# One decoder block with 32 routed experts: the overflow branch ahead of the first expert pair, a hand-ordered router, the last pair's w1 in alternating pieces, and the first FFN splits on the vector engine

## The chip, the cores and the metric

The program runs on one core of a Trainium2 chip. The metric is the device time of one execution in microseconds (us). The kernel before took 915.79 us as the median of three runs (914.03 to 917.89). The engines are named as in the profile: PE is the tensor engine's matrix multiply and PEld its weight load, DVE the vector engine, ACT the scalar engine, POOL the GpSimd engine, and SP the engine whose queue issues the DMAs.

## What is computed

256 tokens of width 1024 pass through two blocks in float32. The first block has a mixer (retention and a gated delta rule), an output projection, and a mixture of experts; the second has a pooling mixer and a convolutional feed-forward network (FFN) of hidden width 2816. The parts that matter here:

```
mod = silu(c) @ w_ada + b_ada                       # shifts, scales, gates
x = x + gate1 * (mix @ w_out)
h2 = modulate(rmsnorm(x), shift2, scale2)
# router: top 1 of 4 groups, then top 2 of the 8 experts in that group
ys = (silu(xs @ w1[e]) * (xs @ w3[e])) @ w2[e]      # for each token's two experts
x = x + gate2 * segment_sum(ys * gate)
x = rmsnorm(x) ; x = x + pool_mixer(rms_norm(x))
x = x + conv_ffn(rms_norm(x))                       # w_in 1024x5632, 3-tap conv, gate, w_out 2816x1024
```

Each of the 32 experts has w1 and w3 of 1024x512 and w2 of 512x1024, 2 MB each, so that the expert weights are 96 matrices of 2 MB, 201 MB, each read once.

## The kernel before

**Experts.** The 32 experts are worked in 16 pairs (the loop over `p`, L1235). A pair holds 64 slots for each of two experts, 128 rows together. `gather(q)` (L1170) serves two pairs: it builds the one-hot matrix OH from `ranks` on DVE, multiplies the normalised tokens with it (32 matmuls, L1183, with the tokens split in a high and a low part, xh and xl), scales and shifts the result into `xg` on ACT and DVE in turn, and then makes the transposed one-hot matrix `oT` and the slot gates `gs` (L1193 to L1200, called the slot rows below). The pair then multiplies xg with w1 and w3 (L1259), forms `hid` (silu on ACT, product with gs on DVE, L1266), transposes it (L1271) and multiplies with w2 (L1282). The result is split in a high and a low part (L1292 on ACT, L1293 on POOL) and added back to the tokens by `scatter` (L1213, L1217), one pair later.

**Weights.** SP's queue loads each weight matrix into a slot of SBUF (2 MB; eight slots, six from pair 12 on, when `load_tail` rearranges the pools). A slot's DMA waits until the matmuls that read the slot's last weights are done. Pair 0's six matrices and pair 1's w1 are loaded ahead of the experts. The pairs 1, 2 and 3 (FINE) load a matrix in four pieces of 512 KB, which wait for the matmuls of the same quarter; pairs 4 to 14 load each in one DMA of 2 MB; the last pair loads w1 in two DMAs of 2 MB, and w3 and w2 in 512 KB pieces that alternate between its two experts (L1245). The order of PE's and SP's instructions inside the pair loop is that of the code (manual schedule, L1233); elsewhere, and on the other engines, a scheduler sets it.

**The overflow branch.** If an expert has more than 64 tokens, `overflow()` (L1126) works the rest of them with plain loops. Each engine loads the largest count (`bigi`) into a register and branches over the body. With the inputs here the body is skipped. It is called after the w1 and w3 matmuls of pair 1 (L1262). On SP its place is behind the pieces of pair 1's weights.

**Router.** Behind the output projection the logits `lg` give the group (L1066 on), the two experts (L1082 on), their probabilities, and by a prefix sum on PE (L1105 to L1110) each token's rank in its expert. `xl`, the low part of the tokens, is two DVE instructions of 128x1024 (L1116). The scheduler orders them.

**The tail.** After the last pair `stats` (L1326) adds the scattered result, forms v3 (x times the final norm's weight, L1330) and the transposed tokens (L1334); POOL scales the pool weights (L1324); PE multiplies (L1360), ACT and DVE scale the result to `zs` (L1366, L1364), PE sums the windows (L1380), and the result of the normalisation (v3, L1391) is transposed (L1402) and split into gh (ACT) and gl (DVE). The FFN multiplies each weight tile in three parts (L288: high with high, low with high, high with low); ACT makes the high part `wh` of a 128x1024 weight tile (L279), and DVE or POOL the low part `wl` (L282). The first FFN weights, four such tiles, are split in the tail, with wl on POOL (L1374).

Of the kernel before, what the change touches and what calls it, by code (L numbers as in the profile page):

```python
# [177 lines left out]
def build(ctx, tc, io, out, dbg=None):  # L178
# [873 lines left out]
    rinv(ss2[:, :, 0], ss2[:, :, 0], D)  # L1052
    for t in range(2):
        S.activation(xh[:, t, :], x1[:, t, :], AF.Copy, scale=ss2[:, t, 0:1])
    lg = mt([128, 2, 40], "lg")
    for t in range(2):
        V.scalar_tensor_tensor(lg[:, t, :], psl[t][:, 0:40], ss2[:, t, 0:1], rbias, op0=ALU.mult, op1=ALU.add)
# [13 lines left out]
    pg = mt([128, 2], "pg")  # L1071
    V.reciprocal(pg, pz)
# [14 lines left out]
    ez = mt([128, 2], "ez")  # L1087
    for t in range(2):
        S.activation(ee[:, t, :], emx[:, t, :], AF.Exp, bias=enm[:, t:t + 1], accum_out=ez[:, t:t + 1])
    V.reciprocal(ez, ez)  # L1090
    pe = mt([128, 2, 2], "pe")
    V.tensor_tensor(pe, ee[:, :, 0:2], ez[:, :, None].to_broadcast([128, 2, 2]), op=ALU.mult)
# [5 lines left out]
    oh = [mt([128, 2, 32], f"oh{i}") for i in range(2)]  # L1098
    for i in range(2):
        V.tensor_tensor(oh[i], io32[:, None, :].to_broadcast([128, 2, 32]),  # L1100
                        ei[:, :, i:i + 1].to_broadcast([128, 2, 32]), op=ALU.is_equal)
    M = mt([128, 2, 32], "M")
    V.tensor_tensor(M, oh[0], oh[1], op=ALU.add)
    psk = bank()
    PE.matmul(psk[:, 0:32], lhsT=cav("ustrict"), rhs=M[:, 0, :], start=True, stop=True)  # L1105
    PE.matmul(psk[:, 32:64], lhsT=cav("ustrict"), rhs=M[:, 1, :], start=True, stop=False)
    PE.matmul(psk[:, 32:64], lhsT=cav("ones"), rhs=M[:, 0, :], start=False, stop=True)
    psn = bank()
    for t in range(2):
        PE.matmul(psn[:, 0:32], lhsT=cav("ones"), rhs=M[:, t, :], start=t == 0, stop=t == 1)  # L1110
# [3 lines left out]
    V.scalar_tensor_tensor(ranks, psk[:, 0:64].rearrange("p (t e) -> p t e", t=2), 1.0, M, op0=ALU.add, op1=ALU.mult)  # L1114
    for t in range(2):
        V.scalar_tensor_tensor(xl[:, t, :], x1[:, t, :], ss2[:, t, 0:1], xh.bitcast(F32)[:, t, :], op0=ALU.mult, op1=ALU.subtract)  # L1116
    dump("ranks", ranks)
    dump("gates", gates)

# [2 lines left out]
    V.tensor_reduce(big, psn[:, 0:32], axis=AX.X, op=ALU.max)  # L1122
    bigi = mt([128, 1], "bigi", dtype=I32)
    V.tensor_copy(bigi, big)

    def overflow():  # L1126
            nmax = nc.values_load(bigi[0:1, 0:1], min_val=0, max_val=T)
            with tc.If(nmax > SLOTS):
                h2T8 = mt([128, 8, T], "h2T", tag="xg")

                def h2T(k):
                    return h2T8[:, k, :]

                for k in range(8):
                    ps = bank()
                    for t in range(2):
                        for x in (xh, xl):
                            PE.matmul(ps[:, 128 * t:128 * t + 128], lhsT=x.bitcast(F32)[:, t, 128 * k:128 * k + 128], rhs=ident,
                                      start=x is xh, stop=x is xl)
                    affine(h2T(k), ps[:, :T], A2[:, k:k + 1], B2[:, k:k + 1])  # L1140
                gov = mt([128, 2, NE], "gov")
                V.tensor_scalar(gov, ranks, float(SLOTS), None, op0=ALU.is_gt)
                V.tensor_tensor(gov, gov, gates, op=ALU.mult)
                with tc.For_i(0, NE, 1) as e:
                    gcol = mt([128, 2], "gcol")
# [23 lines left out]

    def gather(q):  # L1170

        e0 = 4 * q
        OH = mt([128, 2, 4, SLOTS], "OH", dtype=F32R)
        V.tensor_tensor(OH, cav("iota")[:, None, None, 1:65].to_broadcast([128, 2, 4, SLOTS]),
                        ranks[:, :, e0:e0 + 4, None].to_broadcast([128, 2, 4, SLOTS]), op=ALU.is_equal)
        xg = mt([128, 8, 4 * SLOTS], "xg")
        for d2 in range(4):
            ps = bank("pa").rearrange("p (d s) -> p d s", d=2)
            for d in range(2):
                dd = slice(256 * d2 + 128 * d, 256 * d2 + 128 * d + 128)  # L1180
                for t in range(2):
                    for x in (xh, xl):
                        PE.matmul(ps[:, d, :], lhsT=x[:, t, dd], rhs=OH[:, t].rearrange("p g s -> p (g s)"),  # L1183
                                  start=t == 0 and x is xh, stop=t == 1 and x is xl)
            for d in range(2):
                dd = 2 * d2 + d
                affine(xg[:, dd, :], ps[:, d, :], A2[:, dd:dd + 1], B2[:, dd:dd + 1])
        got = []
        for j in range(2):
            pt = bank("pa")  # L1190
# [1 line left out]
            for t in range(2):  # L1192
                PE.transpose(pt[:, 128 * t:128 * t + 128], oh[t], ident)  # L1193
            for t in range(2):
                PE.matmul(pt[:, T:T + 2], lhsT=oh[t], rhs=gates[:, t, e0 + 2 * j:e0 + 2 * j + 2], start=t == 0, stop=t == 1)
# [35 lines left out]
    last = NE // 2 - 1  # L1231
    order = ExitStack()
    order.enter_context(tc.manual_schedule(engines={ENG.PE, ENG.SP}))  # L1233
    nxt = gather(0)
    for p in range(NE // 2):  # L1235
        if p == 12:
            load_tail()
        for nm in ("w1", "w3", "w2"):
            if p == NE // 2 - 1 and nm != "w1":
                k = 4 if nm == "w2" else 8  # L1240
                for g in range(2):
                    wt[p, nm, g] = slot().rearrange("p a n -> p (a n)").rearrange("p (a n) -> p a n", a=k)
# [128 lines left out]
    for i in range(2):  # L1371
# [107 lines left out]
```

## Time and profile before

The profiled execution took 919.07 us; its span, from the first to the last instruction, is 917.0 us. The table is worked out from the views by stretch.

| stretch (us) | what runs | PE busy | DVE busy | DMA |
|---|---|---|---|---|
| 229 to 253 | end of the output projection, router, first gather | 16.55 of 24 | 14.08 | 36 GB/s |
| 253 to 300 | pairs 0 and 1 | 42.62 of 47 | 8.59 | 324 GB/s |
| 350 to 400 | experts | 50.00 of 50 | 12.57 | 428 GB/s |
| 700 to 730 | pool mixer | 22.89 of 30 | 26.57 | 424 GB/s |
| 760 to 917 | FFN | 153.02 of 157 | 90.21 | 109 GB/s |

A busy PE in the experts is not a PE at its peak: a matmul that is overlapped with the next counts as busy. An answer by line gives, for each group of instructions, the busy time, the mean duration of one, and the idle time of the engine just ahead of it with what ended it.

### The profile page before, as it was taken

What the parts mean: (1) busy time and instruction counts of PE and PEld (TensorE: products, weight loads), DVE (VectorE), ACT (ScalarE), POOL (GpSimd) and SP (SyncE); (2) the same over time, 40 slices, a digit from 0 to 9 for tenths busy, and PEclk for the clock granted to TensorE, in tenths of its full rate; (3) what the DMA queues carried; (4) which work ended last, traced back from release to release, by engine and by line L of the source; (5) the groups of instructions that cost most, each with busy time, mean ns of one, the idle gap of its engine ahead of it and who ended that gap; (6) DMA issues with size and microseconds to landing.
All of it is one profiled execution on the core that took longest, in us unless ns stands there. A gap on an engine that the chain in (4) does not pass through costs nothing. (4 is left out here: it accounts for less than half of the span.)

```text
span 917.0 us, 12931 instructions
## 1 busy us (share of the span) xinstructions
PE 849.2 (93%) x5318; PEld 537.2 (59%) x5318; DVE 402.7 (44%) x739; ACT 274.0 (30%) x505; POOL 195.6 (21%) x141
## 2 busy tenths in 40 slices
PE   3988999989698999999898998999999699999998
PEld 1674778768534435353442533435335599999996
DVE  2577588585512123232122321422206775566554
ACT  2342244454510111011011110211104465555552
POOL 0333331261000111100011010100112424513525
PEclk9997999999799999999999999899999999999999
DMA  9972679768069999999999999999999835454001
GB/s 383 420 323 94 277 283 398 293 258 296 33 225 403 409 419 428 427 428 427 428 425 430 426 430 426 405 404 430 427 410 425 374 111 209 151 226 177 1 1 46
DMA packets 30433, 288.53 MB, mean 315 GB/s; under 512 B 3489, under 2 KB 3873, under 8 KB 15393
## 3 DMA queue, kind: packets, MB, share of 16 engines
q1 hardware_dynamic: 30370, 287.66, 76.8%
q8 instruction: 44, 0.72, 0.3%
q14 instruction: 19, 0.16, 0.0%
HBM read 286.60 MB, written 1.05 MB: 314 GB/s over the span
## 5 line engine op out<-in xcount | busy, mean ns | idle before, releaser
L1259 PE MATMUL ps<-wt,xg 128*64 128x512 f32 x1024 | 237.3, 610 | 14.7 <-DMA wt<-in_w 14.6
L1259 PEld LDWEIGHTS ps<-wt,xg 128*64 128x64 f32 x1024 | 77.7, 140 | 171.3 <-issue 146.1
L279 ACT ACTIVATE wh<-wt 128x512 fp32r<-128x512 f32 (+1 forms) x138 | 114.0, 832 | 98.1 <-PE ps L288 87.7
L1293 POOL TENSOR_TENSOR Yl<-Yf,Yh 128x512 fp32r<-128x512 f32 x30 | 38.3, 1275 | 419.0 <-ACT Yh L1292 419.0
L282 POOL TENSOR_TENSOR wl<-wt,wh 128x512 fp32r<-128x512 f32 (+1 forms) x56 | 106.4, 1912 | 98.7 <-ACT wh L279 96.3
L1282 PE MATMUL ps<-wt,hidT 128*64 128x512 f32 x512 | 113.6, 595 | 0.9 <-ACT hidT L208 0.7
L1266 DVE SCALAR_TENSOR_TENSOR hid<-ps,gs,hid 128x512 f32<-128x512 f32 x16 | 12.0, 751 | 230.6 <-PE ps L1259 202.8
L288 PE MATMUL ps<-gh,wh 128*128 128x256 f32 x352 | 98.8, 281 | 1.4 <-ACT gh L1407 1.4
L288 PE MATMUL ps<-gh,wl 128*128 128x256 f32 x352 | 98.9, 281 | 0.0
L288 PE MATMUL ps<-gl,wh 128*128 128x256 f32 x352 | 98.9, 281 | 0.0
L282 DVE TENSOR_TENSOR wl<-wt,wh 128x512 fp32r<-128x512 f32 (+1 forms) x82 | 79.2, 976 | 44.1 <-ACT wh L279 44.0
L1282 PEld LDWEIGHTS ps<-wt,hidT 128*64 128x64 f32 x512 | 37.3, 137 | 66.4 <-issue 59.4
L288 PEld LDWEIGHTS ps<-gh,wl 128*128 128x128 f32 x352 | 67.6, 192 | 0.0
L288 PEld LDWEIGHTS ps<-gh,wh 128*128 128x128 f32 x352 | 66.0, 188 | 1.8 <-ACT gh L1407 1.6
L288 PEld LDWEIGHTS ps<-gl,wh 128*128 128x128 f32 x352 | 66.1, 188 | 0.2
L1287 DVE TENSOR_TENSOR Yf<-ps,g2b 128x512 f32<-128x512 f32 x31 | 21.4, 692 | 82.2 <-PE ps L1282 82.2
L1292 ACT ACTIVATE Yh<-Yf 128x512 fp32r<-128x512 f32 x30 | 18.9, 630 | 112.6 <-DVE Yf L1287 112.6
L1434 DVE SCALAR_TENSOR_TENSOR yf<-ps,sm,yf 128x254 f32<-128x254 f32 x88 | 41.7, 480 | 12.3 <-ACT yf L1431 10.8
L215 ACT ACTIVATE xg<-ps,modT,A 128x256 f32<-128x256 f32 x32 | 18.1, 565 | 93.1 <-PE ps L1183 93.1
L1265 ACT ACTIVATE hid<-ps 128x512 f32<-128x512 f32 x16 | 9.6, 597 | 112.8 <-PE ps L1259 98.1
L1217 DVE TENSOR_TENSOR x<-x,ps 128x512 f32<-128x512 f32 x64 | 41.2, 681 | 1.3 <-PE ps L1210 0.8
L1438 POOL TENSOR_TENSOR yf<-yf 128x256 f32<-128x256 f32 x22 | 19.6, 893 | 85.2 <-ACT yf L1437 85.2
(380 smaller groups left out, 1307.0 us busy)
## 6 DMA issues: line engine op xcount, KB each, us to landing
wt<-in_w SPq DMA_DIRECT2D x76, 2048.0 KB, 27.3
wt<-in_w SPq DMA_DIRECT2D x80, 512.0 KB, 10.2
wt<-in_w_ada SPq DMA_DIRECT2D x12, 2048.0 KB, 10.6
wt<-in_ffn_w_in SPq DMA_DIRECT2D x11, 2048.0 KB, 8.3
wt<-in_w_in SPq DMA_DIRECT2D x7, 2048.0 KB, 14.0
wt<-in_ffn_w_out SPq DMA_DIRECT2D x5, 2048.0 KB, 9.2
wt<-in_w_out SPq DMA_DIRECT2D x2, 2048.0 KB, 7.9
wt<-in_w_in SPq DMA_DIRECT2D x2, 1024.0 KB, 18.9
```

Of the source, the lines that this page charges most:

```text
L215: S.activation(dst, src, AF.Identity, scale=a, bias=b)
L279: S.activation(hi, src, AF.Copy)
L282: (eng or V).tensor_tensor(lo, src, hi.bitcast(F32), op=ALU.subtract)
L288: PE.matmul(ps, lhsT=a, rhs=b, start=first and n == 0, stop=last and n == 2)
L1217: V.tensor_tensor(a, a, ps[t, c], op=ALU.add)
L1259: PE.matmul(ps[64 * g:64 * g + 64, :], lhsT=xg[:, k, 64 * g:64 * g + 64], rhs=wt[p, nm, g][:, k, :], start=k == 0, stop=k == 7)
L1282: PE.matmul(py[c][64 * g:64 * g + 64, :], lhsT=hidT[:, f, 64 * g:64 * g + 64], rhs=wt[p, "w2", g][:, f, 512 * c:512 * c + 512], start=f == ...
L1287: V.tensor_tensor(yf, py[c], g2b[:, 512 * c:512 * c + 512], op=ALU.mult)
L1292: S.activation(yh, yf, AF.Copy)
L1293: G.tensor_tensor(yl, yf, yh.bitcast(F32), op=ALU.subtract)
L1434: V.scalar_tensor_tensor(y[:, sh:], ps[:, :T - sh], cw[:, 3 * m + tap:3 * m + tap + 1], y[:, sh:], op0=ALU.mult, op1=ALU.add)
L1438: G.tensor_tensor(ys[0], ys[0], ys[1], op=ALU.mult)
```

## The change

Five edits, all in the expert stage and the tail.

1. `overflow()` is called ahead of pair 0, behind the first gather and behind the eight 512 KB pieces of pair 1's w3. Its buffers carry other names; its body is the same.
2. DVE's instructions from the logits to `bigi` follow the order of the code. The order in the code is changed: experts, M and the prefix sums first, then the probabilities, `ranks`, the first OH, then xl, the gates and `bigi`.
3. `gather` is cut in three: `hits` (OH), `gather` (xg) and `slot_rows`. A gather multiplies with all of xh before xl: the first one over all eight column blocks, the later ones two blocks at a time. The slot rows of pairs 0 and 1 are made behind pair 0's w1 and w3 matmuls; those of later gathers stay behind the gather.
4. The last pair's w1 is loaded like its w3, in eight pieces of 512 KB that alternate between the two experts.
5. The four first FFN splits make wl on DVE, and stand behind x4 in the code.

```diff
+    hand = ExitStack()
+    hand.enter_context(tc.manual_schedule(engines={ENG.DVE}))
     lg = mt([128, 2, 40], "lg")
...
+    oh = [mt([128, 2, 32], f"oh{i}") for i in range(2)]
...
+    V.tensor_tensor(M, oh[0], oh[1], op=ALU.add)
+    psk = bank("pb")
+    PE.matmul(psk[:, 0:32], lhsT=cav("ustrict"), rhs=M[:, 0, :], start=True, stop=True)
...
+    pg = mt([128, 2], "pg")
+    V.reciprocal(pg, pz)
     V.reciprocal(ez, ez)
...
     V.tensor_tensor(pe, pe, psum_[:, :, None].to_broadcast([128, 2, 2]), op=ALU.mult)
...
+    V.scalar_tensor_tensor(ranks, psk[:, 0:64].rearrange("p (t e) -> p t e", t=2), 1.0, M, op0=ALU.add, op1=ALU.mult)
+    def hits(q):
+        OH = mt([128, 2, 4, SLOTS], "OH", dtype=F32R)
+        V.tensor_tensor(OH, cav("iota")[:, None, None, 1:65].to_broadcast([128, 2, 4, SLOTS]),
+                        ranks[:, :, 4 * q:4 * q + 4, None].to_broadcast([128, 2, 4, SLOTS]), op=ALU.is_equal)
+        return OH
+    OH0 = hits(0)
+    for t in range(2):
+        V.scalar_tensor_tensor(xl[:, t, :], x1[:, t, :], ss2[:, t, 0:1], xh.bitcast(F32)[:, t, :], op0=ALU.mult, op1=ALU.subtract)
     for i in range(2):
         V.tensor_tensor(oh[i], oh[i], pe[:, :, i:i + 1].to_broadcast([128, 2, 32]), op=ALU.mult)
...
+    def gather(q, OH):
         xg = mt([128, 8, 4 * SLOTS], "xg")
+        for d4 in range(0, 8, 2 if q else 8):
+            dn = range(d4, d4 + (2 if q else 8))
+            ps = {d: bank("pa").rearrange("p (d s) -> p d s", d=2) for d in dn[::2]}
+            for x in (xh, xl):
+                for d in dn:
+                    for t in range(2):
+                        PE.matmul(ps[d - d % 2][:, d % 2, :], lhsT=x[:, t, 128 * d:128 * d + 128],
...
-    nxt = gather(0)
+    xg = gather(0, OH0)
+    for key in pairs[8:10]:
+        expert_dma(key, slot(), PIECES)
+    overflow()
     for p in range(NE // 2):
...
         for nm in ("w1", "w3", "w2"):
-            if p == NE // 2 - 1 and nm != "w1":
+            if p == NE // 2 - 1:
...
-        if p == 1:
-            overflow()
+        if not p:
+            rows = slot_rows(0, OH0)
+        oT, gs = rows.pop(0)
...
-        if not nxt and p < last:
-            nxt = gather(p // 2 + 1)
+        if p % 2 and p < last:
+            OH = hits(p // 2 + 1)
+            xg = gather(p // 2 + 1, OH)
+            rows = slot_rows(p // 2 + 1, OH)
...
-    for i in range(2):
-        for vg in range(2):
-            c = 256 * vg + 128 * i
-            pre.append(split(tail_w["split"], w0[:, :, c:c + 128], [128, 8, 128], "w", NSPLIT, G))
...
     dump("x4", x1)
+    for i in range(2):
+        for vg in range(2):
+            c = 256 * vg + 128 * i
+            pre.append(split(tail_w["split"], w0[:, :, c:c + 128], [128, 8, 128], "w", NSPLIT))
```

**PE around pair 0.** Before, from the end of the first gather on (L1193 and L1195 are the slot rows, L1259 the w1 and w3 matmuls, L1282 the w2 matmuls, L1127 and L1128 the branch):

```order
L1193 MATMUL ps<-ca,OH 128x128 x2
L1195 MATMUL ps<-gates,OH 128x2 x2
L1193 MATMUL ps<-ca,OH 128x128 x2
L1195 MATMUL ps<-gates,OH 128x2 x2
L1259 MATMUL ps<-wt,xg 64x512 x32
L1271 MATMUL ps<-ca,hid 128x128 x4
L1282 MATMUL ps<-wt,hidT 64x512 x16
L1259 MATMUL ps<-wt,xg 64x512 x32
L1127 TENSOR_LOAD bigi
L1128 COMPARE_AND_BRANCH
```

Now, the end of the first gather (L1191) and the branch:

```order
L1102 MATMUL ps<-M,ca 128x32 x2
L1191 MATMUL ps<-OH,xh 128x256 x16
L1191 MATMUL ps<-OH,xl 128x256 x16
L1139 TENSOR_LOAD bigi
L1140 COMPARE_AND_BRANCH
```

and, behind the body that is skipped, pair 0 (L1272 w1 and w3, L1204 and L1206 the slot rows, L1298 w2):

```order
L1272 MATMUL ps<-wt,xg 64x512 x32
L1204 MATMUL ps<-ca,OH 128x128 x2
L1206 MATMUL ps<-gates,OH 128x2 x2
L1204 MATMUL ps<-ca,OH 128x128 x2
L1206 MATMUL ps<-gates,OH 128x2 x2
L1285 MATMUL ps<-ca,hid 128x128 x4
L1298 MATMUL ps<-wt,hidT 64x512 x16
```

The branch has moved from behind pair 1's L1259 to between the gather and pair 0, and the slot rows from ahead of pair 0's first matmul to behind its w3.

**SP at the branch.** Before, the 16 pieces are those of pair 1's w3 and w2:

```order
L314 DMA wt<-in_w 128x4096 x5
L314 DMA wt<-in_w 128x1024 x16
L1127 TENSOR_LOAD bigi
L1127 ISA x2
L1128 COMPARE_AND_BRANCH
```

Now only w3's eight pieces stand ahead of it:

```order
L314 DMA wt<-in_w 128x4096 x5
L314 DMA wt<-in_w 128x1024 x8
L1139 TENSOR_LOAD bigi
L1139 ISA x2
L1140 COMPARE_AND_BRANCH
```

The eight pieces of w2, which wait for pair 0's w1 matmuls, now follow the branch.

**DVE in the router.** Now, from the last probability to the branch (before, L1116's two xl instructions stood between em, L1077, and ei, L1083):

```order
L1112 TENSOR_TENSOR pe<-pe,psum__2372 128x4
L1113 SCALAR_TENSOR_TENSOR ranks<-ps,M 128x64
L1118 TENSOR_TENSOR OH<-ca,ranks 128x512
L1124 SCALAR_TENSOR_TENSOR xl<-x_73,ss_2074,xh 128x1024 x2
L1126 TENSOR_TENSOR oh_2354<-oh_2354,pe 128x64
L1126 TENSOR_TENSOR oh_2355<-oh_2355,pe 128x64
L1127 TENSOR_TENSOR gates<-oh_2354,oh_2355 128x64
L1133 TENSOR_REDUCE bigc<-ps 128x1
L1135 CAST bigi<-bigc 128x1
```

xl stands behind OH, and bigi behind xl and the gates; the branch waits for bigi.

## Rows read from the trace of the kernel before

**Rows 1.** The chain that ended last: start, us, what.

```profile
727.88 183.09 PE ps L288 x1311
```

**Rows 2.** Stretches: us, busy per engine (instructions), PE clock, DMA share, GB/s.

```profile
350.00:400.00 50.00, 50.00 (x249) 20.77 (x248) 12.57 (x24) 6.04 (x11) 5.08 (x4) 1.00 1.01 428
235.00:253.50 18.50, 12.38 (x72) 10.97 (x73) 10.98 (x48) 9.10 (x19) 0.00 (x0) 0.64 0.00 1
```

**Rows 3.** Shorter stretches behind the pause in the DMAs.

```profile
254.00:264.00 10.00, 10.00 (x48) 3.30 (x46) 0.00 (x0) 0.60 (x1) 0.00 (x0) 1.00 0.83 246
264.00:268.00 4.00, 2.38 (x14) 0.91 (x12) 0.75 (x1) 0.60 (x1) 0.00 (x0) 1.00 0.99 390
268.00:272.00 4.00, 4.00 (x20) 1.29 (x18) 0.50 (x1) 0.00 (x0) 0.00 (x0) 1.00 0.15 52
272.00:275.00 3.00, 3.00 (x16) 1.01 (x14) 0.20 (x1) 0.63 (x1) 1.27 (x1) 1.00 0.88 292
275.00:285.00 10.00, 10.00 (x48) 3.30 (x46) 0.69 (x1) 0.63 (x1) 1.26 (x1) 1.00 1.02 397
```

**Rows 4.** Waits of SP's queue, 229 to 272: total us, times, longest.

```profile
SPq L314 <- PE ps L1259: 31.2, 4, 27.6
```

**Rows 5.** The branch (L1128) on each engine: ns min/median/max, first and last start us.

```profile
L1128 SPq EVENT_SEMAPHORE  x8: 17/17/17, 263.2 to 270.8; - x8
...
L1128 DVEq COMPARE_BRANCH  x1: 72/72/72, 275.7 to 275.7; - x1
...
L1128 PEldq COMPARE_BRANCH  x1: 6193/6193/6193, 284.8 to 284.8; - x1
```

**Rows 6.** Timeline, behind the branch: start, us, what, idle before it.

```profile
291.28 0.47 PE L1213 MATMUL ps<-Yh,oT 128*128 128x512 f32 x1 [2.66 <-PEq L1128]
```

**Rows 7.** Timeline of the router and pair 0.

```profile
237.73 1.28 DVE L1116 SCALAR_TENSOR_TENSOR xl<-x,ss,xh 128x1024 fp32r<-128x1024 f32 x1
...
241.54 0.17 DVE L1090 RECIPROCAL ez<-ez 128x2 f32<-128x2 f32 x1
...
244.11 0.69 DVE L1174 TENSOR_TENSOR OH<-ca,ranks 128x512 fp32r<-128x512 f32 x1
...
244.95 0.55 PE L1183 MATMUL ps<-OH,xh 128*128 128x256 f32 x1 [1.04 <-DVE bigi L1124]
...
250.30 0.38 PE L1193 MATMUL ps<-ca,OH 128*128 128x128 f32 x2
...
251.56 13.95 PE L1259 MATMUL ps<-wt,xg 128*64 128x512 f32 x64
```

**Rows 8.** Stretches by granted clock, the columns of rows 2.

```profile
234.70:248.20 13.50, 7.38 (x33) 7.15 (x34) 8.10 (x39) 6.05 (x14) 0.00 (x0) 0.50 0.00 0
674.90:678.20 3.30, 3.30 (x10) 0.96 (x8) 0.00 (x0) 0.00 (x0) 0.00 (x0) 0.50 1.03 411
```

**Rows 9.** Timeline of PE in the last pair.

```profile
673.68 15.64 PE L1259 MATMUL ps<-wt,xg 128*64 128x512 f32 x62 [2.14 <-DMA wt<-in_w]
...
692.03 7.09 PE L1282 MATMUL ps<-wt,hidT 128*64 128x512 f32 x32 [0.20 <-DVE hidT L206]
```

**Rows 10.** The last pair's 16 alternating pieces (L1245): start, and time to landing.

```profile
L1245 SPq DMA_DIRECT2D wt<-in_w x16: 327/328/328, 655.2 to 683.9; - x16
...
DMA to landing us min/median/max: 10.2/10.2/21.0
```

**Rows 11.** Timeline of the tail, DVE and then POOL.

```profile
709.94 2.30 DVE L1343 TENSOR_TENSOR s<-s 128x1 f32<-128x1 f32 x1
...
709.74 4.78 POOL L282 TENSOR_TENSOR wl<-wt,wh 128x1024 fp32r<-128x1024 f32 x2 [7.90 <-ACT wh L279]
...
696.88 4.96 POOL L1324 TENSOR_TENSOR pw<-pw,rows 128x512 f32<-128x512 f32 x4 [23.14 <-DMA pw<-in_pool_w]
```

**Rows 12.** Groups by line and shape, tail and FFN: busy us, mean ns.

```profile
L1368 DVE SCALAR_TENSOR_TENSOR x<-v,s,rows 128x1024 f32<-128x1024 f32 x2 | 6.5, 3234 | 0.0
L282 DVE TENSOR_TENSOR wl<-wt,wh 128x1024 fp32r<-128x1024 f32 x40 | 48.9, 1222 | 28.9 <-ACT wh L279 28.9
```

More of the change, by code (lines that the diff above doesn't have):

```diff
@@ L1070, in build @@
         S.activation(ge[:, t, :], lg[:, t, 0:4], AF.Exp, bias=nmx[:, t:t + 1], accum_out=pz[:, t:t + 1])
-    pg = mt([128, 2], "pg")
-    V.reciprocal(pg, pz)
     ohg = mt([128, 2, 4], "ohg")
@@ L1089, in build @@
         S.activation(ee[:, t, :], emx[:, t, :], AF.Exp, bias=enm[:, t:t + 1], accum_out=ez[:, t:t + 1])
+    oh = [mt([128, 2, 32], f"oh{i}") for i in range(2)]
+    for i in range(2):
+        V.tensor_tensor(oh[i], io32[:, None, :].to_broadcast([128, 2, 32]),
+                        ei[:, :, i:i + 1].to_broadcast([128, 2, 32]), op=ALU.is_equal)
+    M = mt([128, 2, 32], "M")
+    V.tensor_tensor(M, oh[0], oh[1], op=ALU.add)
+    psk = bank("pb")
+    PE.matmul(psk[:, 0:32], lhsT=cav("ustrict"), rhs=M[:, 0, :], start=True, stop=True)
+    PE.matmul(psk[:, 32:64], lhsT=cav("ustrict"), rhs=M[:, 1, :], start=True, stop=False)
+    PE.matmul(psk[:, 32:64], lhsT=cav("ones"), rhs=M[:, 0, :], start=False, stop=True)
+    psn = bank("pb")
+    for t in range(2):
+        PE.matmul(psn[:, 0:32], lhsT=cav("ones"), rhs=M[:, t, :], start=t == 0, stop=t == 1)
+    pg = mt([128, 2], "pg")
+    V.reciprocal(pg, pz)
     V.reciprocal(ez, ez)
@@ L1097, in build @@
     V.tensor_tensor(pe, pe, psum_[:, :, None].to_broadcast([128, 2, 2]), op=ALU.mult)
-    oh = [mt([128, 2, 32], f"oh{i}") for i in range(2)]
-    for i in range(2):
[L1100 to L1108, printed above, removed]
+    V.scalar_tensor_tensor(ranks, psk[:, 0:64].rearrange("p (t e) -> p t e", t=2), 1.0, M, op0=ALU.add, op1=ALU.mult)
[5 more added lines that the diff above has]
+    OH0 = hits(0)
     for t in range(2):
-        PE.matmul(psn[:, 0:32], lhsT=cav("ones"), rhs=M[:, t, :], start=t == 0, stop=t == 1)
+        V.scalar_tensor_tensor(xl[:, t, :], x1[:, t, :], ss2[:, t, 0:1], xh.bitcast(F32)[:, t, :], op0=ALU.mult, op1=ALU.subtract)
     for i in range(2):
@@ L1113, in build @@
     V.tensor_tensor(gates, oh[0], oh[1], op=ALU.add)
-    V.scalar_tensor_tensor(ranks, psk[:, 0:64].rearrange("p (t e) -> p t e", t=2), 1.0, M, op0=ALU.add, op1=ALU.mult)
-    for t in range(2):
-        V.scalar_tensor_tensor(xl[:, t, :], x1[:, t, :], ss2[:, t, 0:1], xh.bitcast(F32)[:, t, :], op0=ALU.mult, op1=ALU.subtract)
     dump("ranks", ranks)
@@ L1124, in build @@
     V.tensor_copy(bigi, big)
+    hand.close()
     def overflow():
@@ L1128, in overflow @@
             with tc.If(nmax > SLOTS):
-                h2T8 = mt([128, 8, T], "h2T", tag="xg")
+                h2T4 = [mt([128, 2, T], "h2T", tag=f"Y{i}{c}") for i in "hl" for c in range(2)]
                 def h2T(k):
-                    return h2T8[:, k, :]
+                    return h2T4[k // 2][:, k % 2, :]
                 for k in range(8):
@@ L1167, in overflow, with slot_rows @@
                                 V.tensor_tensor(x1[:, t, cs], x1[:, t, cs], ty, op=ALU.add)
[L1170 to L1175, printed above, removed]
-        xg = mt([128, 8, 4 * SLOTS], "xg")
[L1177 to L1187, printed above, removed]
+    def gather(q, OH):
+        xg = mt([128, 8, 4 * SLOTS], "xg")
+        for d4 in range(0, 8, 2 if q else 8):
[5 more added lines that the diff above has]
+                        PE.matmul(ps[d - d % 2][:, d % 2, :], lhsT=x[:, t, 128 * d:128 * d + 128],
+                                  rhs=OH[:, t].rearrange("p g s -> p (g s)"), start=t == d % 2 == 0 and x is xh, stop=t == d % 2 == 1 and x is xl)
+            for d in dn:
+                affine(xg[:, d, :], ps[d - d % 2][:, d % 2, :], A2[:, d:d + 1], B2[:, d:d + 1])
+        return xg
+    def slot_rows(q, OH):
         got = []
@@ L1194, in gather @@
             for t in range(2):
-                PE.matmul(pt[:, T:T + 2], lhsT=oh[t], rhs=gates[:, t, e0 + 2 * j:e0 + 2 * j + 2], start=t == 0, stop=t == 1)
+                PE.matmul(pt[:, T:T + 2], lhsT=oh[t], rhs=gates[:, t, 4 * q + 2 * j:4 * q + 2 * j + 2], start=t == 0, stop=t == 1)
             oT = mt([128, T], "oT", bufs=3, dtype=F32R)
@@ L1200, in gather @@
                 V.tensor_copy(gs[64 * g:64 * g + 64, :], pt[64 * g:64 * g + 64, T + g:T + g + 1])
-            got.append((xg[:, :, 128 * j:128 * j + 128], oT, gs))
+            got.append((oT, gs))
         return got
@@ L1252, in build @@
             nc.sync.dma_start(tail_w["cp"], io["cp"])
-        xg, oT, gs = nxt.pop(0)
         ph = []
@@ L1258, in build @@
                 for g in range(2):
-                    PE.matmul(ps[64 * g:64 * g + 64, :], lhsT=xg[:, k, 64 * g:64 * g + 64], rhs=wt[p, nm, g][:, k, :],
+                    PE.matmul(ps[64 * g:64 * g + 64, :], lhsT=xg[:, k, 128 * (p % 2) + 64 * g:128 * (p % 2) + 64 * g + 64], rhs=wt[p, nm, g][:, k, :],
                               start=k == 0, stop=k == 7)
             ph.append(ps)
-        if p == 1:
-            overflow()
+        if not p:
+            rows = slot_rows(0, OH0)
+        oT, gs = rows.pop(0)
         hid = mt([128, DE], "hid")
@@ L1370, in build @@
     w0 = wload(io["ffn_w_in"][0], 8, 512)
-    for i in range(2):
-        for vg in range(2):
-            c = 256 * vg + 128 * i
-            pre.append(split(tail_w["split"], w0[:, :, c:c + 128], [128, 8, 128], "w", NSPLIT, G))
     for t in range(2):
@@ L1392, in build @@
     dump("x4", x1)
+    for i in range(2):
+        for vg in range(2):
+            c = 256 * vg + 128 * i
+            pre.append(split(tail_w["split"], w0[:, :, c:c + 128], [128, 8, 128], "w", NSPLIT))
     gh, gl = [], []
```

## The prediction

> **What bounds the kernel now.** The chain of waits comes first: it ends with 183.09 us of PE on L288, unbroken from 727.88 to the end [rows 1]. So the FFN is bound by PE, and whatever happens ahead of 727.88 moves the end one for one; no edit touches the FFN's loop. The views by stretch then say what bounds each stage ahead of it. In the experts the DMAs move 428 GB/s at a share of 1.01 [rows 2]: 200 MB of weights pass through one pipe, and the stage ends when its last byte has landed, plus what PE and DVE do behind it. A gain there is either time in which the pipe ran empty, or work behind the last byte. The pipe runs empty from 235 to 253.5 (1 GB/s) [rows 2], and again from 268 to 272 (52 GB/s), with 292 GB/s to 275 [rows 3]. The waits of SP's queue explain the first: 27.6 us for pair 0's first quarter of w1 [rows 4]. The line of the branch explains the second: SP stands in it with eight semaphore waits from 263.2 to 270.8 [rows 5], and can issue nothing meanwhile. The timelines give the router, the last pair and the tail.
>
> **The change, part by part.** The profiled execution took 919.07 us, which is the span of 917.0 and 2.07 around it; that is 3.28 above the median of the runs. The sum is made on the span, and 3.28 comes off at the end. About 0.5%, 4.6 us, is what a measurement of this kernel can tell from no change.
>
> *The branch, SP's side.* Eight waits of 7.6 us in all drain the DMAs. Against the 397 GB/s behind them [rows 3], the loss is (4 x (397 - 52) + 3 x (397 - 292)) / 397 = 4.3 us. Moved ahead of pair 0, the same waits find pieces of w3, which wait for no matmul of the experts and have landed by 235; they should end at once. What is late next is the release of slots by PE, as now: the first stretch at 246 GB/s (254 to 264) stays. Gain 4.3; bounds 0 (rival 3 below goes lower) and 4.3.
>
> *The branch, PE's side.* The price is that PE's branch now stands ahead of pair 0's first matmul, which releases the slot for which SP waits. Pair 0 starts at 251.56 now [rows 7]. First, how early it could start. DVE has `ez` from ACT at 241.54; six instructions of about 0.2 us then lead to OH at some 242.95 instead of 244.11 [rows 7]. The gather, 244.95 to 250.30, could go 1.15 earlier, but it runs at half clock until 248.2 [rows 8], so I take 0.7: its end at 249.6. The slot rows, 250.30 to 251.56, leave the path, 1.26 us, and xg's last scaling on ACT or DVE takes about half of that place: 250.2 if the branch costs nothing. Second, the branch. `bigi` stands behind OH (242.95 + 0.69), two xl of 1.28, and five small instructions (1.0): 247.2; with the register load 247.7. DVE's compare and branch took 72 ns, PE's 6,193 ns [rows 5], of which PE's matmuls saw 2.66 of idle time [rows 6]. Full price: 247.7 + 6.2 = 253.9. Idle price behind the gather: 249.6 + 2.66 = 252.3. I take 253.0, between the two rows of PE's own branch, with 250.2 and 253.9 as ends: 1.5 later than now, bounds 1.4 earlier and 2.3 later. A pause also costs clock: behind the 2.14 us wait of the last pair, PE had half clock for 3.3 us [rows 8, 9], worth up to 1.65; here I take 0.5, since the first quarter alone sets the restart. Queued behind PE's branch is all of pair 0; SP's pieces wait for it. Term A: 4.3 - 1.5 - 0.5 = +2.3.
>
> The Trainium skill, "Runtime: NRT & Kernel Launch", section "Instruction fetch mechanics", speaks against this edit: a taken branch whose target lies outside the fetched window stalls until its page has come by DMA. PE's 6.19 us agree; no row shows such a fetch with the DMAs idle. By that rule the stall returns at the new place and pair 0 starts near the late end.
>
> *Last pair.* Now PE waits 2.14 us for w1's second 2 MB, starts at 673.68 and runs 15.64 [rows 9], to 689.32; `hid` takes 2.71, to 692.03; w2 takes 7.09, to 699.12. But the last piece was issued at 683.9 and took 10.2, so it landed at 694.1 [rows 10]: PE is 5.0 us behind the DMAs. The 16 pieces cover 673.6 to 694.1, 1.28 us each. Eight such for w1 take 10.24 rather than 4.19 MB / 428 GB/s = 9.8, so landings move 0.45 later: w1 at 674.1, w3 at 684.3, w2 at 694.6. PE now works each quarter as it lands: a matrix takes 13.95 / 2 = 7.0 [rows 7], so w3's last quarter ends at 684.3 + 1.75 = 686.05, `hid` at 688.76, and w2's last quarter at 694.6 + 1.77 = 696.35. Gain 699.12 - 696.35 = 2.8. Bounds: 3.2 without the slower pieces; 1.0 if the waits between pieces leave the last quarter at half clock (1.77 more). Term B: +2.8.
>
> *The tail's splits.* POOL makes two wl of 4.78 together from 709.74, and in that time DVE's 128x1 product takes 2.30 us [rows 11], against 0.17 for 128x2 [rows 7]. The two final products (L1368) take 6.5 together [rows 12]; the same shape takes 1.28 each in the router [rows 7]. If POOL is the cause, 2.13 + 3.94 = 6.07 come free. DVE gets four wl of 1.222 [rows 12], 4.89, all on the path, since DVE is the tail's busiest engine: +1.18. Against it: POOL's scaling of the pool weights (from 696.88, 4.96 us, started by its DMA [rows 11]) does not come earlier, while v3's products come earlier by term B and fall into it. One product stretched as L1368 is (3.23 to 1.28) would cost 1.95; I take a third, 0.65. Term C: +0.5; bounds -4.9 (nothing freed) and +1.2.
>
> The Trainium skill, "SBUF — State Buffer", section "Who interferes with whom", has the rule: GpSimd and VectorE share a port under an exclusive lock, and a DVE instruction with two SBUF inputs waits for it. The 2.30 us beside POOL's wl agree; by the rule both v3 products would wait too, and the term would be nearer to nothing.
>
> *At nothing:* xh before xl in the later gathers, and their cut (PE waits for DMAs there; uncovered, a bank's wait is some 1 us a gather); the body's buffers (never run).
>
> Sum: 2.3 + 2.8 + 0.5 = 5.6. Span 911.4, execution 913.5, and less 3.28: 910.2.
>
> **The rivals.** *1, the branch costs its full price on the start:* pair 0 at 253.9 and 1.65 of half clock leave A = 4.3 - 2.35 - 1.65 = 0.3, sum 3.6: 912.2. For it: 6,193 ns; against: PE's queue runs ahead of its matmuls, so that part is covered. *2, the branch is covered by the gather:* pair 0 at 250.2, no pause, A = 4.3 + 1.35 = 5.6, sum 8.9: 906.9. For it: DVE's 72 ns; against: PE's own row. *3, slower:* the drain let released slots pile up, so that SP then issued many pieces at once. Without it each piece goes as PE releases it, and the pipe could stay in the 246 GB/s of 254 to 264 for a further pair: 12.58 MB take 51.1 us there, 31.7 at 397, so +19.4 less the 5.6: 929.6. It turns the sign from 5.6 / 0.38 = 15 us of such stretch. For it: that row; against: 390 GB/s at 264 to 268 [rows 3], before the drain, and that PE releases a 4.19 MB half pair in 7.0 us, faster than 428 GB/s. *4, the tail does not do what it says:* POOL isn't what stretches DVE, nothing comes free, C = -4.9, sum 0.2: 915.6. For it: L1368 could be slow on its own; against: it would have to be so at the same shape that takes 1.28 elsewhere.
>
> **How the numbers follow.** The forecast has 0.50, with its own range 907.5 to 912.5; rival 1 has 0.20, rival 2 0.17, rival 3 0.05, rival 4 0.08. Range 905 to 915: from rival 2 with 1.7 of B's and C's upper ends, to the middle of rivals 1 and 4 (912.2 plus B's low end, 1.8, and some of C). It leaves out rival 3, most of rival 4 and some edges. Faster means below 911.2: 0.36 of the forecast's 0.50 (5.6 is only 1.0 above the bound), all but 0.01 of rival 2, and 0.08 of rival 1, where B or C are at their upper ends: 0.60. Slower: rival 3 and 0.01 of rival 4: 0.06. The rest, 0.34, is within 0.5%.
>
> **What would show it.** SP: no chain of semaphores of 7 us behind the branch, and no stretch at 52 GB/s near 270; if the rate stays near 246 past 275, rival 3. PE: the idle time ahead of the first w1 matmul and its start, 250.2, 253.0 or 253.9. Last pair: no wait of 2 us for w1, and w2's end some 2 us behind the last landing rather than 5. Tail: the 128x1 product near 0.17, L1368's products near 1.28, and v3's products stretched or not under POOL's scaling. The FFN's 183 us should stand. What would make the prediction wrong: a stretch of empty DMA at another place, or a later start of pair 0 than 253.9.

## The result, and the profile after

The changed kernel took 907.49 us in the median of four runs (907.33 to 908.06), the kernel before 916.84 (four runs): ratio 0.9898, 95% interval 0.9864 to 0.9933. Two later comparisons, each on one chip, gave 911.85 against 916.58 (0.9944, 0.9924 to 0.9965) and 910.61 against 917.39 (0.9935, 0.9917 to 0.9953). So the change saves 5 to 9 us; 5.6 were forecast. The ratios are not the quotients of the medians, and can differ from them by some 0.2%. The terms that make up the sum came out otherwise than forecast.

The profiled execution has a span of 905.8 us, 11.2 less than before. The chain of waits (start, us, what) ends as it did [rows 1]:

```profile
719.75 180.01 PE ps L288 x1311
```

The FFN starts 8.13 us earlier, and its chain is 3.08 us shorter, though no edit touches it. That part turns out below to differ from execution to execution, so it is no part of the change.

*The drain is gone.* The views by stretch in the columns of rows 2, to be held against [rows 3], and the branch (ns min/median/max, first and last start):

```profile
263.00:268.00 5.00, 3.27 (x22) 1.83 (x18) 1.60 (x6) 0.38 (x1) 0.00 (x0) 1.00 1.02 391
268.00:272.00 4.00, 3.06 (x10) 1.18 (x12) 0.70 (x2) 0.60 (x1) 0.00 (x0) 0.65 1.03 416
272.00:275.00 3.00, 3.00 (x16) 0.98 (x14) 0.26 (x1) 0.00 (x0) 0.00 (x0) 0.90 1.02 408
```

```profile
L1140 SPq EVENT_SEMAPHORE  x8: 17/17/17, 249.9 to 250.5; - x8
...
L1140 PEldq COMPARE_BRANCH  x1: 3427/3427/3427, 247.2 to 247.2; - x1
...
L1140 DVEq COMPARE_BRANCH  x1: 72/72/72, 251.1 to 251.1; - x1
```

416 GB/s stand where 52 stood, and SP's eight semaphores pass in 0.6 us instead of 7.6 [rows 5]. PE's own branch took 3.4 us instead of 6.2.

*Pair 0 does not start later.* The timeline of the router and pair 0 (start, us, what, idle before it), against [rows 7]:

```profile
235.84 0.26 DVE L1059 SCALAR_TENSOR_TENSOR lg<-ps,ss,rbias 128x40 f32<-128x40 f32 x1
...
242.67 0.69 DVE L1118 TENSOR_TENSOR OH<-ca,ranks 128x512 fp32r<-128x512 f32 x1
...
247.06 2.79 PE L1191 MATMUL ps<-OH,xl 128*128 128x256 f32 x16
...
250.99 11.38 PE L1272 MATMUL ps<-wt,xg 128*64 128x512 f32 x52 [1.14 <-ACTq L1140]
```

The gather ends at 249.85, PE idles 1.14 us behind it at the branch, and pair 0 starts at 250.99, not at 253.0. The row stops in the middle of pair 0, and it names ACT's queue, which passes its semaphore at the branch last; PE's own branch ended 0.3 us before 250.99. In the six further traces with the branch between the gather and pair 0 PE's queue is named, with 1.23 to 2.04 us in five and 2.47 in the one with the old router.

*The last pair and the tail.* PE (first fence) waits 0.20 us for w3's last piece, and w2 starts as soon as `hid` is transposed, against [rows 9]. On DVE (second fence) the 128x1 product takes 0.14 and 0.15 us and L1384's products 1.27 and 1.28, against [rows 11, 12]; two of v3's products, 1.53 and 1.16, are stretched by POOL's scaling beside them; and four splits of 1.21 are new.

```profile
681.30 1.93 PE L1272 MATMUL ps<-wt,xg 128*64 128x512 f32 x6 [0.20 <-DMA wt<-in_w]
...
685.93 7.52 PE L1298 MATMUL ps<-wt,hidT 128*64 128x512 f32 x32 [0.21 <-DVE hidT L206]
```

```profile
696.93 1.53 DVE L1346 TENSOR_TENSOR v<-x,rows 128x512 f32<-128x512 f32 x1
...
705.26 0.15 DVE L1359 TENSOR_TENSOR s<-s 128x1 f32<-128x1 f32 x1
705.33 1.27 DVE L1384 SCALAR_TENSOR_TENSOR x<-v,s,rows 128x1024 f32<-128x1024 f32 x1
...
706.60 1.21 DVE L282 TENSOR_TENSOR wl<-wt,wh 128x1024 fp32r<-128x1024 f32 x1
```

The whole tail, from the end of w2 to the first FFN matmul, by stretch: before, and then after.

```profile
699.12:727.88 28.76, 21.61 (x97) 16.12 (x97) 25.14 (x44) 15.73 (x40) 13.16 (x7) 0.94 1.01 427
```

```profile
693.45:719.75 26.30, 20.33 (x98) 15.24 (x97) 24.36 (x48) 15.93 (x40) 5.42 (x4) 1.00 1.01 428
```

DVE is busy 0.78 us less (third number), but its idle time fell as well, from 3.62 to 1.94: that is how 2.46 us went.

### The profile page after: what moved, and what is told of

Its sections match the earlier page's. It is cut to its first block, busy times and chain, and to the rows that moved or that the text cites. A ratio compares the mean times of both kernels' runs of the same rounds, so it can differ in the third digit from the quotient of the medians.

```text
span 905.8 us, 12941 instructions
## 1 busy us (share of the span) xinstructions
PE 848.4 (94%) x5318; PEld 541.4 (60%) x5318; DVE 402.0 (44%) x743; ACT 273.9 (30%) x505; POOL 185.7 (21%) x137
## 3 DMA queue, kind: packets, MB, share of 16 engines
HBM read 286.60 MB, written 1.05 MB: 318 GB/s over the span
## 4 chain that ended last, share of the span: by engine, by line
PE 53%; DMA 16%; DVE 3%; issue 0%; ACT 0%; SPq 0%; DVEq 0%; ACTq 0%
PE ps L288 20%; DMA wt<-in_w 16%; PE ps L1272 15%; PE ps L1298 10%; PE ps L1191 3%; PE ps L1224 2%; PE ps L1034 1%; PE ps L1206 1%; PE ps L1285 1%; DVE wl L282 0%; PE ps L1204 0%; PE ps L1221 0%; DVE x L1478 0%; DVE dT L1350 0%; DVE x L1228 0%
## 5 line engine op out<-in xcount | busy, mean ns | idle before, releaser
L1272 PE MATMUL ps<-wt,xg 128*64 128x512 f32 x1024 | 237.7, 607 | 9.3 <-DMA wt<-in_w 7.9
L1272 PEld LDWEIGHTS ps<-wt,xg 128*64 128x64 f32 x1024 | 81.3, 140 | 162.4 <-issue 142.8
L1298 PE MATMUL ps<-wt,hidT 128*64 128x512 f32 x512 | 116.1, 602 | 0.9 <-ACT hidT L208 0.7
L282 POOL TENSOR_TENSOR wl<-wt,wh 128x512 fp32r<-128x512 f32 (+1 forms) x52 | 96.0, 1860 | 86.4 <-ACT wh L279 84.1
L282 DVE TENSOR_TENSOR wl<-wt,wh 128x1024 fp32r<-128x1024 f32 (+1 forms) x86 | 84.0, 986 | 43.0 <-ACT wh L279 42.4
L1298 PEld LDWEIGHTS ps<-wt,hidT 128*64 128x64 f32 x512 | 41.7, 138 | 64.5 <-issue 54.3
## 6 DMA issues: line engine op xcount, KB each, us to landing
wt<-in_w SPq DMA_DIRECT2D x88, 512.0 KB, 10.2
```

The costliest lines, as they stand in the source:

```text
L282: (eng or V).tensor_tensor(lo, src, hi.bitcast(F32), op=ALU.subtract)
L1272: PE.matmul(ps[64 * g:64 * g + 64, :], lhsT=xg[:, k, 128 * (p % 2) + 64 * g:128 * (p % 2) + 64 * g + 64], rhs=wt[p, nm, g][:, k, :], start ...
L1298: PE.matmul(py[c][64 * g:64 * g + 64, :], lhsT=hidT[:, f, 64 * g:64 * g + 64], rhs=wt[p, "w2", g][:, f, 512 * c:512 * c + 512], start=f == ...
```

## The experiments

Two numbers are used across the traces. The *lead* is how much earlier than in the first trace of before the same number of weight bytes had landed (summed over the DMA packets): at 85 MB, behind the drain, at 200 and 230 MB, ahead of and behind pair 12, and at 240 MB, early in the last pair. The *logits* are the start of `lg`, 235.62 before: the front ends up to 2.8 us earlier or 0.9 later in other executions of the same code, so starts are counted from there.

**Branch alone.** In the kernel before (the buffers of the skipped body change their names as well):

```diff
     nxt = gather(0)
+    for key in pairs[8:10]:
+        expert_dma(key, slot(), PIECES)
+    overflow()
...
-        if p == 1:
-            overflow()
```

> The kernel before with edit 1 alone: pair 1's w3 pieces and the overflow branch stand ahead of pair 0, behind the whole first gather and its slot rows. Theory (the drain): SP's eight waits of 7.6 us behind the branch vanish, the weight stream has no stretch at 52 GB/s near 270 and runs 4.0 to 4.5 us ahead of before from 288 on; the last landing moves by what of that survives pair 12, at least 2.5; time 2.5 to 4.5 us less. Rival (the branch on the start path): PE's first w1 matmul comes 1 to 3 us later than 251.56 and the gain is under 1.5 us. On the FFN chain, which took 183.1 us before and 180.0 in the changed kernel: 180 here if it belongs to this edit, 183 if to another, and neither if it differs from program to program.

916.17 against 916.40: ratio 1.0000 (0.9978 to 1.0022). Its two places, the branch and pair 0:

```profile
L1128 PEldq COMPARE_BRANCH  x1: 3527/3527/3527, 248.3 to 248.3; - x1
```

```profile
251.96 15.65 PE L1262 MATMUL ps<-wt,xg 128*64 128x512 f32 x64 [2.47 <-PEq L1128]
```

The drain went, but PE idles 2.47 us, starts pair 0 18.46 us behind the logits (15.94 before), and then runs its 64 matmuls in 15.65 us instead of 13.95, since a stretch at half clock follows the pause. The lead at 85 MB is 2.44, of which 2.12 is the earlier front. That is rival 1, at its full price: the branch on the start path eats the drain.

**Last pair's w1 alone.** In the kernel before:

```diff
-            if p == NE // 2 - 1 and nm != "w1":
+            if p == NE // 2 - 1:
```

> The kernel before with edit 4 alone: the last pair's w1 in eight alternating pieces of 512 KB. Theory (term B): no wait of 2.14 us for w1, the last landing 0.45 later, w2's last matmul ends 2.0 to 2.8 us earlier than 699.12, time 2 to 3 us less. Rival: the pieces cost the stream as much as PE gains, so w2's end moves by under 1 us. FFN chain 183.1 if it does not belong to this edit, 180 if it does.

915.48: ratio 0.9993 (0.9972 to 1.0014). Its stream loses 0.4 us in the last pair, as the term had it (0.45). w2 ended at 697.55, 1.57 earlier than before, but 0.79 of that is lead at 240 MB: by this measure 0.8 us belong to the edit (1.4 by a better one, below), and then the tail takes 29.72 us instead of 28.76, with v3's first product at 1.27 us beside POOL's scaling.

**First FFN splits alone.** In the kernel before, the four `pre.append(split(...))` moved behind x4 without the argument G (as in the change's diff).

> The kernel before with edit 5 alone: the low parts of the first four FFN tiles on DVE behind x4, instead of on POOL. Theory (POOL stretches DVE): the 128x1 product falls from 2.30 to 0.15 us, the two final products from 6.5 to 2.5 in all, the tail from w2's end to the first FFN matmul from 28.76 to 26 to 27.5, time 1.2 to 2.7 us less; v3's products stay at 0.69 since POOL's scaling still ends before them. Rival (POOL is not the cause): the products stay long and the four splits add 4.9 us: time 1 to 5 us more. FFN chain 183.1 if it does not belong to this edit, 180 if it does.

908.99: ratio 0.9931 (0.9895 to 0.9967). Its DVE timeline:

```profile
712.85 0.15 DVE L1343 TENSOR_TENSOR s<-s 128x1 f32<-128x1 f32 x1
712.92 1.27 DVE L1368 SCALAR_TENSOR_TENSOR x<-v,s,rows 128x1024 f32<-128x1024 f32 x1
```

With the wl gone from POOL, nothing stretches these products. The tail takes 26.01 us. Over all traces the tail is 28.8 to 29.7 in the five without this edit, 26.0 to 26.7 in the nine with it: 2.9 us between their means. The time fell by more, 6.3 us by the ratio; the traced execution was the longest of the five (915.35), and what else the short ones saved is not shown.

**Router and gather alone** (the changed kernel with the branch, the w1 pieces and the splits undone).

> The changed kernel with edits 1, 4 and 5 undone, so the kernel before with the hand order on DVE, the gather in three parts and the slot rows behind pair 0's w1 and w3. Theory: the first gather starts 1.4 us earlier and pair 0, with no branch ahead of it and no slot rows, at about 249.9 instead of 251.56: 1.5 us off everything behind; the drain stays; time 1 to 2 us less. Rival: xh ahead of xl costs the later gathers what the start gains: no change. FFN chain 183.1 if it does not belong to this edit, 180 if it does.

911.60: ratio 0.9970 (0.9944 to 0.9997), 2.7 us; the medians differ by 4.8. Pair 0 starts 13.82 us behind the logits, 2.1 less than before: the router gains more than the 1.35 forecast for a branch that costs nothing. The drain stands (SP's branch waits 8.4 us) and eats half of it: the lead at 85 MB, less the earlier logits, is 1.27, against 0.27 on average in the four traces with the old router and the branch at its old place.

**Without the branch** (the changed kernel, `overflow()` left out).

> The changed kernel without the overflow branch: the tokens past 64 of an expert are left out, which these inputs don't have. It prices the branch at its new place. Theory (the branch costs what PE idles ahead of pair 0): the first w1 matmul starts at 249.8 to 250.0 instead of 250.99, 1.0 to 1.2 us earlier relative to the gather's end, the stream follows by the same, time 0.5 to 1.5 us less than the changed kernel. Rival (the branch's page of code comes by DMA and costs more than PE's idle time, on SP, ACT or DVE too): 2.5 us or more less.

903.03: ratio 0.9842 (0.9817 to 0.9866). Pair 0 starts 13.80 us behind the logits, against 15.15 to 15.75 in five traces with the branch behind the new router's gather: it costs PE 1.4 to 2.0 us at the start. A sixth, the first with the spread broadcasts below, has 14.48, with a shorter stretch at half clock in its router. The lead at 85 MB, less the earlier logits, is 6.5, against 3.2 to 5.8, 4.3 on average, in the six. In time the forecast of 0.5 to 1.5 us missed and the rival's 2.5 or more came, but the start shows only what the theory priced, and a little more. The rest of the 8.8 us between its time and the 911.85 beside it is not explained by that, and stays open.

**The changed kernel twice more, and the one before.** The FFN chain:

> The changed kernel once more, beside the kernel before on the same chip. What is asked is the FFN chain, 183.1 us in the trace of before and 180.0 in that of the changed kernel, with 117.8 and 113.4 ns from one 128x256 matmul to the next. Theory (the pitch differs from execution to execution, not with the change): the chain is anywhere from 178 to 185 and the runs spread over some 5 us, as those of before did. Rival (the pitch belongs to the change): 113 ns again, and all runs within 1 us of 907.5.

> The kernel before once more, for its trace. Theory (the pitch differs from execution to execution): 113 or 118 ns, the chain 178 to 185 us. Rival (it belongs to the kernel): 118 ns and 183 us again. The drain behind the branch and the two holes in the weight stream stand as before in either case.

> The changed kernel a third time, as the partner of the three others on this chip. Theory: 4 to 9 us less than the kernel before (0.990 to 0.996); the FFN chain takes about 180 or about 184 us, 113 or 118 ns from one 128x256 matmul to the next, as the execution falls. Rival (the first four runs, at 907.3 to 908.1, were the rule): 0.989 to 0.991.

The second trace of the kernel before has 180.64 us:

```profile
727.81 180.64 PE ps L288 x1311
```

The FFN's 128x256 matmuls follow each other at 0.12 us in the first trace of before and at 0.11 to 0.12 in the second, of the same program (start, us, what):

```profile
759.75 0.28 PE L288 MATMUL ps<-gh,wh 128*128 128x256 f32 x1
...
760.34 0.28 PE L288 MATMUL ps<-gh,wl 128*128 128x256 f32 x1
760.46 0.28 PE L288 MATMUL ps<-gh,wh 128*128 128x256 f32 x1
760.58 0.28 PE L288 MATMUL ps<-gl,wh 128*128 128x256 f32 x1
```

```profile
759.81 0.28 PE L288 MATMUL ps<-gl,wh 128*128 128x256 f32 x1
...
760.38 0.28 PE L288 MATMUL ps<-gh,wh 128*128 128x256 f32 x1
760.49 0.28 PE L288 MATMUL ps<-gl,wh 128*128 128x256 f32 x1
```

Seven steps take 0.83 us in the first, six take 0.68 in the second: 118 and 113 ns, at a granted clock of 1.00 in both. Of 14 traces three have 118 (before, the w1 pieces alone, the one without the branch) and eleven 113, and nothing in between; over the 1,056 such matmuls that is about 4.7 us. It follows no edit. What sets it was not found. All three traces of the changed kernel had 113, and their times still spread from 907.3 to 914.4.

**The changed kernel with w1 whole** (the w1 edit undone).

> The changed kernel with edit 4 undone: the last pair's w1 in two DMAs of 2 MB. Theory (term B was mis-sized; of the 2.8 us only what is left by a w2 pass that runs whole behind w3's last piece): w2's last matmul ends 0 to 1.5 us later, relative to the stream, than in the changed kernel, and the time is within 1.5 us of it. Rival (term B as predicted): 2.3 to 3 us later and 2 to 3 us more time.

910.40, beside 910.61 for the changed kernel on that chip: ratios 0.9941 (0.9919 to 0.9963) and 0.9935. In the traces, w2's end less the lead at 240 MB is 0.1 to 2.5 us earlier than before in the eight traces with the pieces (mean 1.7), and between 0.9 earlier and 0.2 later in the six without.

That spread is not in PE's work. In the changed kernel's first trace the last piece was issued at 681.3 and took 10.2 us, so it landed at 691.5:

```profile
L1259 SPq DMA_DIRECT2D wt<-in_w x24: 327/328/427, 644.2 to 681.3; - x24
...
DMA to landing us min/median/max: 10.2/10.2/19.6
```

w2 ended at 693.45, 2.0 us behind it. Held against its own last landing in this way, w2 ends 1.97 to 2.10 us behind in all eight traces with the pieces, 3.34 to 3.37 in five of the six without, and 5.02 only in the first trace of before, the one whose w1 and w3 matmuls took 15.64 us with a stretch at half clock (13.95 in the five). So the edit is worth 1.4 us behind the stream, and what varies is when the last pieces land.

**A better version: load_tail's broadcasts spread.** The lead falls by up to 4.9 us between 200 and 230 MB in some kernels and not in others, with nothing changed there. The stretches at this place in the changed kernel (the third number from the end is the granted clock, the last GB/s):

```profile
578.00:584.00 6.00, 6.00 (x20) 2.17 (x15) 2.03 (x3) 1.91 (x4) 2.78 (x2) 0.93 0.85 322
584.00:594.00 10.00, 10.00 (x23) 2.90 (x23) 1.38 (x2) 0.60 (x1) 0.00 (x0) 0.53 1.02 433
594.00:600.00 6.00, 6.00 (x32) 1.96 (x30) 0.00 (x0) 0.60 (x1) 0.00 (x0) 1.00 0.67 246
```

Twelve broadcast matmuls stand ahead of pair 12's w1; PE is at half clock from 583 to 593, and the DMAs starve from 594 on; that the late release of slots joins the two is argued, not shown by a row. The edit:

```diff
     def load_tail():
...
-        for i in range(6):
-            ps = bank("pa")
-            PE.matmul(ps, lhsT=cav("ones")[0:1, :], rhs=rf[0:1, 512 * i:512 * i + 512], start=True, stop=True)
-            copy(rf[:, 512 * i:512 * i + 512], ps)
+        tail_w["rf"] = rf
...
         prev = oT, Y
+        if 12 <= p < last:
...
+            for i in range(2 * p - 24, 2 * p - 22):
...
```

> The changed kernel with the six broadcasts of load_tail's rows (12 matmuls of 1x512, 7.6 us ahead of pair 12's first matmul) spread as two behind each of the pairs 12, 13 and 14. Theory (those matmuls delay pair 12's w1 and w3, and with them the release of the two slots for which SP waits): the stream's holes at 580 to 583 and 596 to 600, 3.7 us together, shrink to under 1.5, the last landing comes 2 to 4 us earlier, time 2 to 4 us less than the changed kernel. Rival (the hole is made by the loss of two slots, whatever PE does): the stream stands as in the changed kernel, no change.

> The changed kernel with load_tail's broadcasts spread over the pairs 12 to 14, once more. Theory (the broadcasts make the hole at pair 12): the stream gains 0.5 to 1.5 us on the kernel before between 571 and 644 us, where the changed kernel lost up to 1.5; time 2 to 4 us less than the changed kernel. Rival (the 902.5 us came from the router's half clock, which was shorter in that execution): no difference to the changed kernel that its interval tells.

902.51 (0.9866, 0.9824 to 0.9908) beside 911.85 for the changed kernel, and in a second comparison 908.98 (0.9909, 0.9891 to 0.9928) beside 910.61 (0.9935, 0.9917 to 0.9953): these intervals overlap, so the second comparison alone does not tell the two apart. The same place in the second trace:

```profile
577.00:583.00 6.00, 6.00 (x30) 2.01 (x28) 2.50 (x3) 1.26 (x2) 1.66 (x2) 1.00 0.90 333
583.00:593.00 10.00, 9.27 (x42) 2.92 (x40) 0.00 (x0) 0.60 (x1) 1.12 (x1) 1.00 0.98 418
593.00:599.00 6.00, 6.00 (x28) 2.73 (x24) 2.07 (x4) 0.59 (x1) 0.00 (x0) 1.00 1.00 429
```

The hole behind 594 is gone (429 for 246 GB/s); the one ahead of 583 stays (333 for 322). The lead grows by 0.9 to 1.05 us there in all three traces with this edit; in the other eleven it changes by +0.2 to -4.9, -1.4 on average. So traces with and without the edit differ by some 2.4 us. How much of that is the broadcasts' is not shown: the trace with -4.9 (w1 whole) loses most of it ahead of them, at 199 GB/s and full clock from 577 to 583. By the first comparison it is the fastest version run that computes everything; the first trace also had its logits 2.8 us early and a shorter stretch at half clock in the router, which is no effect of the edit.

**The branch inside the gather** (with the spread broadcasts; `bigi` ahead of xl on DVE, `overflow()` between the xh and the xl matmuls).

> The kernel with the spread broadcasts, and the branch moved into the first gather, between its xh and its xl matmuls, with bigi ahead of xl on DVE. Theory (PE's branch then runs beside the xh matmuls, and xl is ready by its end): PE idles 0 to 0.8 us inside the gather and not behind it, pair 0 starts 0.5 to 1.3 us earlier relative to the logits than in the changed kernel (15.2 to 15.6 us), time 0.5 to 1.3 us less than the kernel with the spread broadcasts alone. Rival (the branch costs 3.4 us or more wherever PE stands): the xl matmuls wait, and pair 0 starts later.

908.59 (0.9911, 0.9893 to 0.9928): no gain over 908.98. PE at the new place:

```profile
247.68 3.75 PE L1194 MATMUL ps<-OH,xl 128*128 128x256 f32 x16 [0.86 <-PEq L1137]
```

The branch took 3.61 us again, PE idles 0.86 inside the gather, and the xl matmuls take 3.75 us at half clock instead of 2.79: pair 0 starts 15.84 us behind the logits, no earlier. The rival was right: the price did not fall at that place.

## Why the prediction was right, point by point

- **Drain, 4.3.** Right in place, and nearly in size: from pair 0's start to 85 MB the first trace of the changed kernel gains 4.45, and seven further ones with the branch moved or left out behind the new router gain 2.4 to 4.4 (3.6 on average in the eight).
- **Pair 0's start, 1.5 later and half clock 0.5.** Wrong, on the good side. It starts 15.15 to 15.75 us behind the logits in five traces (14.48 in a sixth), against 15.9 in three of the four traces with the old router (15.26 in the fourth): 0.2 to 0.8 earlier. The router gained 2.1 and not 1.35: the gather ends 0.9 earlier and the slot rows' 1.26 leave the path whole, since the scaling of xg was no wait of its own. And PE's branch cost 1.4 to 2.0, since it takes 3.3 to 3.8 us in the eight traces where it stands ahead of pair 0 and the weights' DMAs rest, against 6.1 to 6.6 beside them [rows 5]. Half clock fell into pair 0 in one of the three traces of the changed kernel (its 64 matmuls took 15.65 us instead of 13.96) and with the branch alone (15.65), so the loss is 1.7 us or nothing, and not 0.5. Nor does a pause cost clock each time, as the forecast had it: five traces wait 2.2 to 2.5 us for the last pair's w1 and go on at full clock. Term A is some 4.1 us on average (mean of six traces, less the mean of the four with the old order) instead of 2.3; single traces lie 1 us or more to either side. The branch alone shows how near rival 1 was: with the old router the two cancel.
- **Last pair, 2.8.** Right in the order of events, too large in size: 1.4. w2 ends 2.0 to 2.1 us behind the last landing, as the forecast had it (one quarter, 1.77). But the 5.0 that it was held against came from one execution: the 15.64 us of [rows 9] held a stretch at half clock, and the five other traces without the pieces, at full clock, have 3.34 to 3.37. With 3.35 in its place the same sum gives 1.1. The ratios of the two comparisons give 0.6 and 0.5 us (0.9993; 0.9941 less 0.9935), known to some 2 us.
- **Tail, 0.5.** Too small: 2.9. What POOL's end frees was right (6.1), and v3's products do fall into the scaling, 1.3 us instead of 0.65. But the four splits, "all on the path", were not: the tail has 1.7 us less of DVE idle time than before, so part of their 4.8 us fell into it.
- **FFN's 183 us should stand.** It did not in the trace, and that is no effect of the change.
- **Given back:** pair 12's hole cost the first trace 1.5 us of its lead; the other traces without the spread broadcasts change by +0.2 to -4.9 there. The forecast had no such term.
- **Rivals.** Rival 2's time, 906.9, is nearest to the first 907.49, but not by its mechanism: the branch is not covered, PE idles 1.1 to 2.0 us at it. Rival 3 is out, with 391 to 416 GB/s from 263 to 275 where it had 246; so is rival 4, with 1.27 and 1.28 us for L1384's products.

The terms as measured, 4.1 + 1.4 + 2.9 = 8.4, lie above the two later comparisons (4.7 and 6.8 by the medians) and below the first (9.4). The forecast's 5.6 was a sum of terms of which two were too small, A and the tail by 4.2 together, and one too large, the last pair by 1.4. That the total came as near as it did is in part luck: the errors partly cancel, and single executions of one kernel differ by more than the forecast's distance from the result.

The Trainium skill, "Runtime: NRT & Kernel Launch", section "Instruction fetch mechanics", says a branch out of the fetched window waits for its page by DMA. With the DMAs otherwise idle, the changed kernel's trace shows one such transfer on the first instruction queue between 247 and 250.6, while PE stands in the branch:

```profile
q8 instruction: 1, 0.02, 1.8%
```

That agrees with the rule; but the kernel without the branch has one between 245 and 249 too, so this row alone does not prove that PE waits for the transfer. The packets of all 13 traces with a branch say more. Each has exactly one 16 KB packet of this queue inside PE's branch, and the branch ends 1.36 to 1.54 us behind that packet, wherever it falls. The packet takes 1.0 to 1.45 us. It starts 1.0 to 1.3 us after the branch's start where the weights' DMAs rest, and 3.6 to 4.0 us after it where they move 405 to 409 GB/s. So the branch ends with the packet, and the 6.1 to 6.6 us beside the weights are longer than the 3.3 to 3.8 by a later start of it.

## What to carry to other kernels

A drain that was moved is worth what the waiting engine does not lose at its new place: the branch alone gained nothing, the faster router alone 1 us of lead, and both together some 4. Price an engine's work added to a busy tail against its idle time there, not against its busy share. And before a term of 2 to 4 us is read from one trace, look at a second trace of the same kernel: the clock's stretches and the FFN's pace moved single stages by as much.

## What the runs showed of the hardware that was not expected

- The pace of 128x256 matmuls is either 113 or 118 ns at the same granted clock of 1.00, for the whole FFN of an execution, in the same program.
- PE's branch takes 3.3 to 3.8 us in eight traces with the weights' DMAs idle, 6.1 to 6.6 in the five at its old place beside them, and it ends 1.4 to 1.5 us behind the one packet of the instruction queue that falls into it; those of DVE, POOL, ACT and SP 0.05 to 0.07.
- The router's stretch at half clock lasted 13.7 us in eleven traces, 10.2 in two, and 17.1 with the branch inside the gather; in one of the two the gather ended 12.43 us behind the logits instead of 13.9. The router's length is thus partly a matter of where that stretch falls.
